# Turning the second tile's normed rows on chip: one edit to a hybrid decoder layer in float32

## The chip, the cores and the metric

The kernel runs on one core of one Trainium2 chip. A core has TensorE (PE, matrix products and 128x128 transposes), VectorE (DVE), ScalarE (ACT), GpSimd (POOL) and SyncE (SP), which work at the same time and wait for each other through semaphores. Transfers between the chip's memory (DRAM here) and the on-chip buffers go through 16 DMA engines; SP, ACT and POOL can issue them, each from its own queue in program order. The metric is the device time of one execution in microseconds; less is better. It is the median of 3 runs.

## What is computed

One decoder layer on 2048 tokens of 1024 channels in float32: a mixing half (RMS norm, one input projection, sliding-window attention, a convolution group, an output projection, RMS norm, residual) and then a SwiGLU half. Only the passage between the halves and the SwiGLU half matter here:

```
h  = h + rms_norm(mixed, mix_post_g)
hn = rms_norm(h, ffn_pre_g)
ff = (silu(hn @ w_gate) * (hn @ w_up)) @ w_down
h  = h + rms_norm(ff, ffn_post_g)
```

## The kernel before, in words

**Tiles and pairs.** The tokens are cut into 4 tiles (w = 0 to 3) of 512 tokens, and the SwiGLU half works on pairs: tiles 0 and 1, then tiles 2 and 3. Each pair's product with the weights is a 2 by 2 block product done with 7 block products in place of 8 (Winograd's form). Its right-hand operands are made from the normed rows `hn`, turned so that channels lie on partitions: B11 and B21 are the lower and upper 512 channels of the pair's first tile, B12 and B22 those of its second tile, and T1 = B12 - B11, T2 = B22 - T1, T3 = B22 - B12, T4 = B21 - T2. Each operand is 4 column blocks k = 0 to 3 of 128 channels by 512 tokens. For exactness each is split into a high part (a copy by ACT) and a low part (a subtraction by DVE, `lo`), and one float32 product becomes 3 matmuls; a block product (`product`) is 4 blocks x 3 = 12 matmuls of 128x512.

**Stages.** `stage_a` projects the inputs, `stage_b` does attention, `stage_taps` and `stage_tail` the convolution, `stage_w` the output projection, and `norm_w`, at its end, both norms of a tile. `stage_pre` (label F) then does the products that need only the pair's first tile (B11 for one half of its steps, B21 for the other): 40 for the first pair, of which the first 8 are done inside `stage_w(1)`, and 32 for the second. `stage_p1` does the others, which need T1, T2, T3, B22 and T4 in this order; `stage_p2` (label G) is the product with `w_down`, whose results go through `finish` (norm, residual from `h_scr`, output).

**How the second tile's rows get turned.** `norm_w` leaves four tiles `xs` of normed rows (128 tokens x 1024 channels each). For the first tile of a pair (w = 0 and 2) `turn_row` takes a block k: four transposes on PE into a PSUM bank, a copy by ACT that applies the gain `g_ffn` into a `gb` buffer, and a DMA into `hT` in DRAM. For the second tile (w = 1 and 3) the four `xs` are written to `hn_scr` in DRAM (L797, ACT's queue). `stage_h_sums` (label H) later loads from it, per k, two column strips of 128 channels (`load_cols`, L820), turns them with PE (`turned`, L842, banks of the pool `tr`), and makes r and t, the sums that become T1 to T4, with 4 `scalar_tensor_tensor` straight from PSUM and one subtraction on DVE; ACT copies B12 and B22 out of PSUM (L885, L887). The first tile's blocks come back from `hT` as `own` (L879).

**Buffers.** `BUFS` (L64 on) sets how many buffers a tag has. Those that matter: `chl` has 5, `mid` 4, `hl` 8, `gb` 2, `raw` 2 (weights, two products' worth each); PSUM has 4 `mm` banks, 3 `tr`, and one `ct`, which `turn_row` uses. `chl` holds, one after the other: `gb` (gain rows) and the four `xs` of `norm_w`, the four `ht` rows that `finish` loads from `h_scr` (L1141), then `own`, `r` and `t` of the sums, then `r1`, `s12`, `s34` of `stage_p1`. The accumulators of `stage_w(1)` and `stage_w(3)` are `mid`.

**Order of the work.** The Python code emits instructions into a main line (`run`) and into lanes: a lane emits a step of its item when the main line's clock has moved on by so much; `lh.rates` and the conditions in `add` set pace and start, `until` forces an item out. Emission order is priority only. The compiler then simulates the program and fixes each engine's order, and with it the order in SP's queue: a DMA whose buffer is not free holds up those behind it, also the weights' (`raw`, L931). The lane `lh` does the sums of the first pair as `S0`, from the step `P0.22` of `stage_pre` on at rate 0.9, and those of the second as `S2`, from `P2.16` on.

Of the kernel before, what the change touches and what calls it, by code (L numbers as in the profile page):

```python
# [12 lines left out]
F32 = mybir.dt.float32  # L13
# [4 lines left out]
AF = mybir.ActivationFunctionType  # L18
ALU = mybir.AluOpType
# [3 lines left out]
S = 2048  # L23
D = 1024
DFF = 2816
P = 128
T = 512
# [10 lines left out]
def layer_kernel(ctx, tc, x, xT, cols, rows, sinks, relb, onehot, w_in, w_pw, w_out, w_gate, w_up, w_down, out):  # L38
    nc = tc.nc
# [39 lines left out]
    act = nc.scalar.activation  # L79
# [38 lines left out]
    stt = dve(nc.vector.scalar_tensor_tensor)  # L118
    vtt = dve(nc.vector.tensor_tensor)
# [74 lines left out]
    ident = cst.tile([P, P], F32, name="ident")  # L194
# [16 lines left out]
    g_ffn = colt[:, 8:16]  # L211
# [27 lines left out]


    glu_scr = dr.tile([4, P, S], F32, name="glu_scr")
    hn_scr = dr.tile([S, D], F32, name="hn_scr")
# [517 lines left out]
    def norm_w(w, acc):  # L760
        L = f"W{w}"
        lab[0] = L

        def whole(src):
            t = f4("chl")
            nc.sync.dma_start(t, src)
            return t

        gb = whole(rows[0].partition_broadcast(P))
        ssq = sm(4)  # L770
        for s in range(4):
            act(junk, acc[s], AF.Square, accum_out=ssq[:, s : s + 1])
            yield 0.75
            lab[0] = L
        r = rsqrt(ssq, 4, D, w < 3)
        xs = [whole(x[w * T + s * P : w * T + (s + 1) * P]) for s in range(4)]
        ssq2 = sm(4)
        yield 3
        for s in range(4):
            lab[0] = L  # L780
            stt(acc[s], acc[s], r[:, s : s + 1], gb, ALU.mult, ALU.mult)
            yield 1.25
            lab[0] = L
            vtt(acc[s], xs[s], acc[s], ALU.add)
            r0 = w * T + s * P
            nc.sync.dma_start(h_scr[r0 : r0 + P], acc[s])
            act(junk, acc[s], AF.Square, accum_out=ssq2[:, s : s + 1])
            yield 1.25
        lab[0] = L
        r2 = rsqrt(ssq2, 4, D, w < 3)  # L790
        yield 3
        for s in range(4):
            lab[0] = L
            act(xs[s], acc[s], AF.Copy, scale=r2[:, s : s + 1])
            if w % 2:
                r0 = w * T + s * P
                nc.scalar.dma_start(hn_scr[r0 : r0 + P], xs[s])  # L797
            yield 1.25
        if w == 0:
            normed.extend(xs)  # L800
        if w == 2:
            for k in range(KC):
                turn_row(w, xs, k)
                yield 2.0

    normed = []

    def turn_row(w, xs, k):
        lab[0] = f"H{w}"
        b = ct()  # L810
        for s in range(4):
            nc.tensor.transpose(b[:, s * P : (s + 1) * P], xs[s][:, k * P : (k + 1) * P], ident)
        u = f2("gb")
        act(u, b, AF.Copy, scale=g_ffn[:, k : k + 1])
        nc.scalar.dma_start(hT[w // 2][k], u)
        return u

    def load_cols(w, k, tag):
        t = f2(tag, (P, 4, P))
        nc.sync.dma_start(t, hn_scr[w * T : (w + 1) * T, k * P : (k + 1) * P].rearrange("(s p) c -> p s c", p=P))  # L820
        return t

    def split_f(x, w):
        act(w[:, 0], x, AF.Copy)  # L824
# [2 lines left out]
    def lo(x, w, on_pool):  # L827
        (ptt if on_pool else vtt)(w[:, 1], x, w[:, 0].bitcast(F32), ALU.subtract)
# [1 line left out]
    OPTAG = {  # L830
        0: dict(B11=["x"] * 4, B21=["hl"] * 4, T1=["mid", "mid", "mb", "mb"], T2=["ql"] * 4, T3=["p"] * 4,
                T4=["yt", "yt", "mid", "mid"], B22=["hl"] * 4),
        2: dict(B11=["ql"] * 4, B21=["mid"] * 4, T1=["hl"] * 4, T2=["hl"] * 4, T3=["x"] * 4,
                T4=["yt", "yt", "mb", "mb"], B22=["p"] * 4),
    }
    COLTAG = {0: ["fc", "at", "fc", "at"], 2: ["fc", "at", "fc", "at"]}

    def turned(w, k, bank_of, tag):
        c = load_cols(w, k, tag)
        b = bank_of()  # L840
        for s in range(4):
            nc.tensor.transpose(b[:, s * P : (s + 1) * P], c[:, s], ident)  # L842
        return b
# [12 lines left out]
    def stage_h_plain(ws, ops, n, off):  # L856
        L = f"H{ws[0]}"
        for k in range(4):
            lab[0] = L
            if ws[0]:  # L860
                u = f2(COLTAG[ws[0]][k])
                nc.sync.dma_start(u, hT[ws[0] // 2][k + off])
            else:
                u = turn_row(0, normed, k + off)
                lab[0] = L
            o = op_tile(ws, ops, n, k, {})
            act(o[:, 0], u, AF.Copy)
            lo(u, o, False)
            yield 2.0

    def stage_h_sums(ws, ops):
        L = f"H{ws[0]}"
        spare = {}
        for k in range(4):
            lab[0] = L
            ct_ = COLTAG[ws[0]]
            g1, g2 = g_ffn[:, k : k + 1], g_ffn[:, k + 4 : k + 5]
            own = t_("chl", (P, 2, T))
            nc.sync.dma_start(own, hT[ws[0] // 2][k :: 4].rearrange("j p t -> p j t"))  # L879
            own = own[:, 0], own[:, 1]  # L880
            b12 = turned(ws[1], k, tr, ct_[2])
            b22 = turned(ws[1], k + 4, tr, ct_[3])
            r = t_("chl", (P, 2, T))
            t = t_("chl", (P, 2, T))
            act(r[:, 1], b12, AF.Copy, scale=g1)  # L885
            b = op_tile(ws, ops, "B22", k, spare)
            act(b[:, 0], b22, AF.Copy, scale=g2)  # L887
            yield 1.5
            lab[0] = L
            stt(r[:, 0], b12, g1, own[0], ALU.mult, ALU.subtract)  # L890
            stt(t[:, 0], b22, g2, r[:, 0], ALU.mult, ALU.subtract)
            stt(r[:, 1], b22, g2, r[:, 1], ALU.mult, ALU.subtract)
            stt(b[:, 1], b22, g2, b[:, 0].bitcast(F32), ALU.mult, ALU.subtract)
            vtt(t[:, 1], own[1], t[:, 0], ALU.subtract)
            yield 3
            for n, x in (("T1", r[:, 0]), ("T2", t[:, 0]), ("T3", r[:, 1]), ("T4", t[:, 1])):
# [406 lines left out]
    def since(lane, name, dt):  # L1303
        return name in lane.done and clk[0] >= lane.done[name] + dt
# [55 lines left out]
    W_LEAD = 4.0  # L1360
    RT = 0.2
    RP = 0.1
    NS = 12
    TIE = 5
    AHEAD = 3
    PRES = {0: 20, 2: 16}
    Q0 = 8
    POOL_LO = (3, 6)
    PRE_S0, PRE_S2 = 22, 16
# [7 lines left out]
    lu = Lane(0.6, 0)  # L1377
    ld = Lane(2.0, 0)
    lanes = [lb, lc, lu, lw, ld, lf, lh, lt]
    lh.rates = {"N1": 1.2, "S0": 0.9, "H0": 1.2}  # L1380
    lf.rates = {n: 0.6 for n in ("O0.1", "O0.3", "E0.1", "E0.3")} | {n: 1.2 for n in ("Y0", "Y1", "O2.1", "O2.3")}
    lc.rates = {"T0": RC0, "T1": RC1, "T2": RC2, "T3": RP}
    lw.rates = {"W0": RW0, "C2": RW, "W2": RW, "C3": RW, "W3": RW}
# [63 lines left out]
    ws, ops = (0, 1), {}  # L1447
# [12 lines left out]
    ws, ops = (2, 3), {}  # L1460
# [76 lines left out]
```

## Time and profile before

| what | before |
|---|---|
| median of 3 runs | 1987.95 us (1983.87 to 1989.76) |
| the profiled execution's own time | 1988.28 us |
| its span in the trace | 1986.6 us |
| TensorE busy | 1933.8 us, 97% of the span |
| VectorE busy | 1469.8 us, 74% |
| ScalarE busy | 957.8 us, 48% |
| GpSimd busy | 292.4 us, 15% |
| mean DMA rate over the span | 224 GB/s |

Times in the trace count from the start of the span. A row of windows has the window, its length, then for PE, PEld (weight loads), DVE, ACT and POOL the busy time with the number of instructions, the clock that PE was granted (1.00 is full), the busy share of the DMA engines and GB/s. A row of the timeline has start, duration, engine (SPq and ACTq are the issuing queues), line, instruction, written tile and read tiles with the stage's label behind @, the number merged, and in brackets how long the engine idled before and what released it. Rows of a tile's view have min, median and max duration in ns and the first and last start. Matmuls overlap in their pipeline, so that PE counts as busy at less than its full rate: the number of matmuls in a window says more than the busy time.

### The profile page before, as it was taken

The page shows a single profiled execution, that of the slowest core. Times are in us where ns is not written, and L with a number is a line of the kernel's source. Part 1 is how long each engine was busy: PE and PEld are TensorE (multiplying, and loading weights), DVE is VectorE, ACT ScalarE, POOL GpSimd, SP SyncE. Part 2 cuts the span into 40 slices and gives each one's busy share as a digit, 9 for nine tenths or more (in the row PEclk, how much of TensorE's full clock was granted, in tenths as well). Part 3 has the DMA queues.
Part 4 walks back from the last instruction along what each step waited for, and adds up shares of the span by engine and source line. Part 5 has one row for each costly group of instructions (what it writes and reads, how often), then busy time and mean ns, then how long its engine had stood idle before and what let it go on. Part 6 is the DMA issues. An engine that isn't in the chain of part 4 may idle for free.

```text
span 1986.6 us, 26668 instructions
## 1 busy us (share of the span) xinstructions
PE 1933.8 (97%) x8730; PEld 1549.4 (78%) x8730; DVE 1469.8 (74%) x2648; ACT 957.8 (48%) x1878; POOL 292.4 (15%) x427
## 2 busy tenths in 40 slices
PE   8999999999998999989999999998999999999997
PEld 6777777777776788778888878886788888888886
DVE  4999969995875898787759965667866665455557
ACT  5455454447646643334345464656643433345443
POOL 4011111111121011220000100000023332311003
PEclk9999999999998999999999999999999999999999
DMA  8786667566659777785478776769844442466664
GB/s 304 251 311 214 211 192 251 181 211 218 221 196 324 267 253 241 252 279 172 140 253 275 256 272 229 249 219 372 295 148 163 170 151 83 143 226 198 212 194 145
DMA packets 219180, 444.07 MB, mean 224 GB/s; under 512 B 22137, under 2 KB 47905, under 8 KB 219041
## 3 DMA queue, kind: packets, MB, share of 16 engines
q1 hardware_dynamic: 200096, 406.71, 61.3%
q0 software_dynamic: 7040, 23.07, 3.4%
q10 hardware_dynamic: 11904, 12.59, 1.8%
q8 instruction: 68, 1.11, 0.2%
q14 instruction: 72, 0.58, 0.1%
HBM read 327.46 MB, written 114.83 MB: 223 GB/s over the span
## 4 chain that ended last, share of the span: by engine, by line
PE 75%; DMA 10%; DVE 9%; issue 3%; ACT 2%; POOL 1%; SPq 0%; DVEq 0%; POOLq 0%; ACTq 0%
PE mm@F L85 30%; PE mm@G L85 16%; PE mm@A L85 14%; PE mm@W L85 5%; PE tr@B L85 4%; DVE fc@C L94 3%; PE tr@W L85 2%; DMA raw@F<-w_gate 1%; PE mm@U L85 1%; DMA chl@G<-h_scr 1%; DMA gb@F<-keeps 1%; DMA td<-wx@G 1%; DVE w@F L94 1%; DMA raw@F<-w_up 1%; DMA raw@A<-w_in 1%
## 5 line engine op out<-in xcount | busy, mean ns | idle before, releaser
L94 DVE SCALAR_TENSOR_TENSOR fc@C<-glu@C,colt,fc@C 128x512 f32<-128x512 f32 x480 | 357.2, 758 | 2.8
L85 PE MATMUL mm@F<-hl@H,w@F 128*128 128x512 f32 x1056 | 259.1, 397 | 8.4 <-ACT mm@F L954 7.8
L85 PEld LDWEIGHTS mm@F<-hl@H,w@F 128*128 128x128 f32 x1056 | 202.2, 192 | 53.1 <-ACT mm@F L954 9.2
L85 PE MATMUL mm@G<-hl@G,hl@G 128*128 128x512 f32 x924 | 227.4, 393 | 1.1 <-DVE hl@G L94 1.1
L824 ACT ACTIVATE w@F<-chl@F 128x512 fp32r<-128x512 f32 x220 | 136.0, 625 | 175.0 <-PE mm@F L85 170.1
L85 PE MATMUL mm@A<-hl@A,w@A 128*128 128x512 f32 x840 | 207.9, 395 | 4.7 <-ACT w@A L127 1.8
L85 PEld LDWEIGHTS mm@G<-hl@G,hl@G 128*128 128x128 f32 x924 | 171.7, 188 | 37.6 <-DVE hl@G L94 1.9
L85 PE MATMUL mm@G<-w@G,hl@G 128*128 128x512 f32 x876 | 199.4, 389 | 0.0
L85 PEld LDWEIGHTS mm@G<-w@G,hl@G 128*128 128x128 f32 x876 | 164.4, 188 | 34.1
L85 PEld LDWEIGHTS mm@A<-hl@A,w@A 128*128 128x128 f32 x840 | 155.4, 188 | 42.9 <-issue 3.1
L94 DVE TENSOR_TENSOR w@F<-chl@F,w@F 128x512 fp32r<-128x512 f32 x198 | 147.4, 747 | 32.9 <-ACT w@F L824 32.5
L85 PE MATMUL mm@F<-mid@H,w@F 128*128 128x512 f32 x528 | 138.9, 412 | 13.4 <-ACT mm@F L954 10.0
L85 PEld LDWEIGHTS mm@F<-mid@H,w@F 128*128 128x128 f32 x528 | 104.8, 200 | 38.2 <-ACT mm@F L954 11.4
L85 PE MATMUL mm@F<-ql@H,w@F 128*128 128x512 f32 x528 | 129.2, 390 | 0.7 <-DVE w@F L94 0.5
L85 PE MATMUL mm@F<-p@H,w@F 128*128 128x512 f32 x528 | 129.0, 390 | 0.0
L85 PE MATMUL mm@F<-x@H,w@F 128*128 128x512 f32 x528 | 126.9, 392 | 0.0
L85 PEld LDWEIGHTS mm@F<-ql@H,w@F 128*128 128x128 f32 x528 | 99.2, 188 | 22.1 <-DVE w@F L94 0.9
L85 PEld LDWEIGHTS mm@F<-p@H,w@F 128*128 128x128 f32 x528 | 99.2, 188 | 20.6
L85 PEld LDWEIGHTS mm@F<-x@H,w@F 128*128 128x128 f32 x528 | 98.5, 188 | 21.0 <-issue 0.8
L127 ACT ACTIVATE w@A<-raw@A 128x512 fp32r<-128x512 f32 x110 | 67.6, 626 | 92.2 <-PE mm@A L85 62.6
L94 DVE TENSOR_TENSOR w@G<-raw@G,w@G 128x512 fp32r<-128x512 f32 x73 | 52.0, 713 | 67.8 <-ACT w@G L824 66.9
L495 POOL TENSOR_SCALAR_AFFINE_SELECT p@B<-p@B 128x512 f32<-128x512 f32 x62 | 52.4, 854 | 337.6 <-ACT p@B L493 336.2
(303 smaller groups left out, 3267.9 us busy)
## 6 DMA issues: line engine op xcount, KB each, us to landing
mids<-fa@F SPq DMA_DIRECT2D x154, 256.0 KB, 3.1
raw@A<-w_in SPq DMA_DIRECT2D x55, 512.0 KB, 4.5
w@A<-lo_in SPq DMA_DIRECT2D x84, 256.0 KB, 3.4
fc@G<-mids SPq DMA_DIRECT2D x77, 256.0 KB, 3.5
fa@G<-mids SPq DMA_DIRECT2D x75, 256.0 KB, 4.8
gb@F<-keeps SPq DMA_DIRECT2D x72, 256.0 KB, 4.2
w@W<-fold SPq DMA_DIRECT2D x32, 512.0 KB, 5.3
chl@F<-w_gate SPq DMA_DIRECT2D x22, 512.0 KB, 4.3
```

The lines of the kernel that those rows point to most:

```text
L85: r = nc.tensor.matmul(*args, **kw)
L94: r = op(*args, **kw)
L127: act(w[:, 0], raw, AF.Copy)
L495: nc.gpsimd.affine_select(out=pg[:, kb].rearrange("p (i q) -> p i q", q=P), in_=pg[:, 1].rearrange("p (i q) -> p i q", q=P), compare_op=AL ...
L824: act(w[:, 0], x, AF.Copy)
```

## The change

`hn_scr` is gone. `norm_w` of the second tile of a pair goes on, after its last scaling, with 8 turns: for k = 0 to 3 it takes a `mid` buffer and turns the blocks k and k + 4 into its two halves with `turn_row`, so that the gain is applied by the copy. The four buffers are kept in `normed`. `stage_h_sums` takes the buffer of its k, and makes the four sums on DVE from on-chip buffers, in `own` and in one more `chl` buffer `r` (`t` is gone); the copy of B22 is now a plain copy, and its low part the usual subtraction. The DMA into `hT` moves from `turn_row` to its callers. Second pair: B21 goes into `hl` buffers and T1 into `mid` (they were the other way round). In the lanes: `S0` starts when `N1` (the norm of tile 1 with its 8 turns) has been emitted, at rate 0.8; `B21.2` starts at `P2.0` at rate 0.5; `S2` starts at `P2.8` if `E0.3` (the last `finish` of the first pair) has been emitted, at rate 0.8.

```
         for s in range(4):
             act(xs[s], acc[s], AF.Copy, scale=r2[:, s : s + 1])
-            if w % 2:
-                r0 = w * T + s * P
-                nc.scalar.dma_start(hn_scr[r0 : r0 + P], xs[s])
             yield 1.25
         if w == 0:
             normed.extend(xs)
-        if w == 2:
+        elif w == 2:
             for k in range(KC):
-                turn_row(w, xs, k)
+                u = turn_row(w, xs, k, f2("gb"))
+                nc.scalar.dma_start(hT[1][k], u)
                 yield 2.0
+        else:
+            for k in range(4):
+                t = t_("mid", (P, 2, T))
+                for j in range(2):
+                    turn_row(w, xs, k + 4 * j, t[:, j])
+                    yield 2.0
+                normed.append(t)
...
-        2: dict(B11=["ql"] * 4, B21=["mid"] * 4, T1=["hl"] * 4, T2=["hl"] * 4, T3=["x"] * 4,
+        2: dict(B11=["ql"] * 4, B21=["hl"] * 4, T1=["mid"] * 4, T2=["hl"] * 4, T3=["x"] * 4,
...
             own = t_("chl", (P, 2, T))
-            nc.sync.dma_start(own, hT[ws[0] // 2][k :: 4].rearrange("j p t -> p j t"))
-            own = own[:, 0], own[:, 1]
-            b12 = turned(ws[1], k, tr, ct_[2])
-            b22 = turned(ws[1], k + 4, tr, ct_[3])
-            r = t_("chl", (P, 2, T))
-            t = t_("chl", (P, 2, T))
-            act(r[:, 1], b12, AF.Copy, scale=g1)
-            b = op_tile(ws, ops, "B22", k, spare)
-            act(b[:, 0], b22, AF.Copy, scale=g2)
-            yield 1.5
-            lab[0] = L
-            stt(r[:, 0], b12, g1, own[0], ALU.mult, ALU.subtract)
-            stt(t[:, 0], b22, g2, r[:, 0], ALU.mult, ALU.subtract)
-            stt(r[:, 1], b22, g2, r[:, 1], ALU.mult, ALU.subtract)
-            stt(b[:, 1], b22, g2, b[:, 0].bitcast(F32), ALU.mult, ALU.subtract)
-            vtt(t[:, 1], own[1], t[:, 0], ALU.subtract)
-            yield 3
+            nc.sync.dma_start(own, hT[ws[0] // 2][k::4].rearrange("j p t -> p j t"))
+            other = normed[k]
+            yield 2.5
+            lab[0] = L
+            b = op_tile(ws, ops, "B22", k, spare)
+            act(b[:, 0], other[:, 1], AF.Copy)
+            r = t_("chl", (P, 2, T))
+            vtt(r[:, 0], other[:, 0], own[:, 0], ALU.subtract)
+            vtt(r[:, 1], other[:, 1], r[:, 0], ALU.subtract)
+            vtt(own[:, 0], other[:, 1], other[:, 0], ALU.subtract)
+            lo(other[:, 1], b, False)
+            vtt(own[:, 1], own[:, 1], r[:, 1], ALU.subtract)
+            yield 2
...
-    lh.rates = {"N1": 1.2, "S0": 0.9, "H0": 1.2}
+    lh.rates = {"N1": 1.2, "S0": 0.8, "B21.2": 0.5, "S2": 0.8}
...
-    lh.add("S0", stage_h_sums(ws, ops), lambda: f"P0.{PRE_S0}" in started and "B3" in lb.done)
+    del normed[:]
+    lh.add("S0", stage_h_sums(ws, ops), lambda: "N1" in lh.done)
...
-    lh.add("B21.2", stage_h_plain(ws, ops, "B21", 4), lambda: since(lw, "N3", NS))
-    lh.add("S2", stage_h_sums(ws, ops), lambda: f"P2.{PRE_S2}" in started)
+    del normed[:4]
+    lh.add("B21.2", stage_h_plain(ws, ops, "B21", 4), lambda: "P2.0" in started)
+    lh.add("S2", stage_h_sums(ws, ops), lambda: f"P2.{PRE_S2}" in started and "E0.3" in lf.done)
```

More of the change, by code (lines that the diff above doesn't have):

```diff
@@ L241, in layer_kernel @@
     glu_scr = dr.tile([4, P, S], F32, name="glu_scr")
-    hn_scr = dr.tile([S, D], F32, name="hn_scr")
     y_scr = dr.tile([4, P, S], F32, name="y_scr")
@@ L800, in norm_w, with turn_row @@
             normed.extend(xs)
-        if w == 2:
+        elif w == 2:
             for k in range(KC):
-                turn_row(w, xs, k)
+                u = turn_row(w, xs, k, f2("gb"))
+                nc.scalar.dma_start(hT[1][k], u)
                 yield 2.0
+        else:
[5 more added lines that the diff above has]
+                normed.append(t)
     normed = []
-    def turn_row(w, xs, k):
+    def turn_row(w, xs, k, u):
         lab[0] = f"H{w}"
@@ L812, in turn_row @@
             nc.tensor.transpose(b[:, s * P : (s + 1) * P], xs[s][:, k * P : (k + 1) * P], ident)
-        u = f2("gb")
         act(u, b, AF.Copy, scale=g_ffn[:, k : k + 1])
-        nc.scalar.dma_start(hT[w // 2][k], u)
         return u
[L818 to L821, printed above, removed]
     def split_f(x, w):
@@ L836, in layer_kernel @@
     COLTAG = {0: ["fc", "at", "fc", "at"], 2: ["fc", "at", "fc", "at"]}
[L838 to L843, printed above, removed]
     def op_tile(ws, ops, n, k, spare):
@@ L863, in stage_h_plain @@
             else:
-                u = turn_row(0, normed, k + off)
+                u = turn_row(0, normed, k + off, f2("gb"))
                 lab[0] = L
+                nc.scalar.dma_start(hT[0][k + off], u)
             o = op_tile(ws, ops, n, k, {})
@@ L875, in stage_h_sums @@
             lab[0] = L
-            ct_ = COLTAG[ws[0]]
-            g1, g2 = g_ffn[:, k : k + 1], g_ffn[:, k + 4 : k + 5]
             own = t_("chl", (P, 2, T))
-            nc.sync.dma_start(own, hT[ws[0] // 2][k :: 4].rearrange("j p t -> p j t"))
-            own = own[:, 0], own[:, 1]
-            b12 = turned(ws[1], k, tr, ct_[2])
-            b22 = turned(ws[1], k + 4, tr, ct_[3])
-            r = t_("chl", (P, 2, T))
-            t = t_("chl", (P, 2, T))
-            act(r[:, 1], b12, AF.Copy, scale=g1)
-            b = op_tile(ws, ops, "B22", k, spare)
-            act(b[:, 0], b22, AF.Copy, scale=g2)
-            yield 1.5
-            lab[0] = L
-            stt(r[:, 0], b12, g1, own[0], ALU.mult, ALU.subtract)
-            stt(t[:, 0], b22, g2, r[:, 0], ALU.mult, ALU.subtract)
-            stt(r[:, 1], b22, g2, r[:, 1], ALU.mult, ALU.subtract)
-            stt(b[:, 1], b22, g2, b[:, 0].bitcast(F32), ALU.mult, ALU.subtract)
-            vtt(t[:, 1], own[1], t[:, 0], ALU.subtract)
-            yield 3
-            for n, x in (("T1", r[:, 0]), ("T2", t[:, 0]), ("T3", r[:, 1]), ("T4", t[:, 1])):
+            nc.sync.dma_start(own, hT[ws[0] // 2][k::4].rearrange("j p t -> p j t"))
[4 more added lines that the diff above has]
+            act(b[:, 0], other[:, 1], AF.Copy)
+            r = t_("chl", (P, 2, T))
+            vtt(r[:, 0], other[:, 0], own[:, 0], ALU.subtract)
[4 more added lines that the diff above has]
+            yield 2
+            for n, x in (("T1", r[:, 0]), ("T2", r[:, 1]), ("T3", own[:, 0]), ("T4", own[:, 1])):
                 lab[0] = L
@@ L1362, in layer_kernel @@
     RP = 0.1
-    NS = 12
     TIE = 5
@@ L1368, in layer_kernel @@
     POOL_LO = (3, 6)
-    PRE_S0, PRE_S2 = 22, 16
+    PRE_S2 = 8
     H1, H2, H3, H4 = 0, 4, 7, 11
```

## The prediction

> **What bounds the kernel now.** I read the page first, then who PE waits for, then windows over the two passages that the change touches, and the timelines of each engine in them.
>
> ```profile
> span 1986.6 us, 26668 instructions
> PE 1933.8 (97%) x8730; PEld 1549.4 (78%) x8730; DVE 1469.8 (74%) x2648; ACT 957.8 (48%) x1878; POOL 292.4 (15%) x427
> ...
> PE mm@F L85 <- ACT mm@F L954: 17.8, 7, 4.2
> ```
>
> PE sets the time: whatever doesn't let PE start a matmul earlier is worth nothing. Its longest wait, 17.8 us in 7 pieces, is in `stage_pre`, for the copy that seeds a PSUM bank. All 7 lie in two windows, from about product 11 of the first pair and product 0 of the second up to the first product of `stage_p1`. A window of undisturbed work stands beside them.
>
> ```profile
> 587.50:685.29 97.79, 89.22 (x378) 72.22 (x377) 69.46 (x105) 61.24 (x107) 6.11 (x14) 0.93 0.88 291
> 1321.82:1432.88 111.06, 98.96 (x417) 79.71 (x416) 87.97 (x187) 75.47 (x146) 1.28 (x1) 0.92 0.99 347
> 1455.00:1555.00 100.00, 100.00 (x443) 82.83 (x442) 70.75 (x84) 38.44 (x67) 35.00 (x23) 1.00 0.48 164
> ```
>
> Undisturbed, a matmul takes 100/443 = 0.2257 us. Each of the two windows has 32 transposes, in 8 groups at about 0.4 us a group (below). So the first needs 346 x 0.2257 + 3.2 = 81.3 us and takes 97.8; the second needs 385 x 0.2257 + 3.2 = 90.1 and takes 111.1. **16.5 and 21.0 us are lost**, 37.5 in all. The DMA engines are 0.88 and 0.99 busy there, against 0.48 undisturbed. Part of the loss is clock: 24 matmuls behind a wait of 3.76 us take 8.33 us, where 24 x 0.2257 = 5.4.
>
> ```profile
> 624.27 8.54 PE L85 MATMUL mm@F<-hl@H,w@F 128*128 128x512 f32 x24 [3.41 <-ACT mm@F L954]
> ...
> 685.29 1.52 PE L85 MATMUL mm@F<-ql@H,w@F 128*128 128x512 f32 x6
> ...
> 1386.33 8.33 PE L85 MATMUL mm@F<-mid@H,w@F 128*128 128x512 f32 x24 [3.76 <-ACT mm@F L954]
> ...
> 1432.88 7.87 PE L85 MATMUL mm@F<-hl@H,w@F 128*128 128x512 f32 x34
> ```
>
> The rows at 685.29 and 1432.88 are the first products of `stage_p1`; they are the two dates that count.
>
> **What goes.**
>
> ```profile
> hn_scr<-chl@W ACTq DMA_DIRECT2D x8, 512.0 KB, 7.1
> ...
> fc@H<-hn_scr SPq DMA_DIRECT2D x8, 256.0 KB, 5.4
> at@H<-hn_scr SPq DMA_DIRECT2D x8, 256.0 KB, 5.4
> ```
>
> 4 MB go in and 4 MB out of `hn_scr`, 4.2 MB per pair in decimal units. In the second window, where the DMA engines move 347 GB/s and have no room, that is 12.1 us of transfer, and up to 12.1 of its 21.0 us can come back. In the first, with 0.88, PE would be the limit without them and all 16.5 can come back. If nothing new stood in the way, the sum would be -16.5 - 12.1 = -28.6 us.
>
> **What the work costs.** The transposes are 32 per pair before and after. The next rows have DVE and ACT.
>
> ```profile
> L94 DVE SCALAR_TENSOR_TENSOR chl@H<-tr@H,colt,chl@H 128x512 f32<-128x512 f32 x24 | 17.2, 746 | 4.5 <-ACT chl@H L885 2.9 <-DMA chl@H<-hT 0.7 <-DVE chl@H L94 0.5
> L94 DVE TENSOR_TENSOR chl@H<-chl@H,chl@H 128x512 f32<-128x512 f32 x8 | 5.5, 685 | 0.0
> ...
> L814 ACT ACTIVATE gb@H<-ct@H,colt 128x512 f32<-128x512 f32 x16 | 11.0, 686 | 11.2 <-PE ct@H L812 11.1
> L885 ACT ACTIVATE chl@H<-tr@H,colt 128x512 f32<-128x512 f32 x8 | 5.4, 676 | 3.3 <-DVE p@G L94 3.3
> ...
> L867 ACT ACTIVATE hl@H<-gb@H 128x512 fp32r<-128x512 f32 x4 | 2.5, 630 | 0.8 <-ACT gb@H L814 0.8
> ```
>
> DVE does 5 subtractions per k, 5 x 0.685 = 3.4 us, in place of 4 x 0.746 + 0.685 = 3.7: 1 us less per pair. ACT has 8 turn copies of 0.686 for 8 of 0.676, and 4 plain copies of 0.63 more: 2.6 us more per pair. Both are busy for 61 to 88 us of the windows' 98 and 111, so I cost this at 0; without that cover it would be +2.6 - 1 per pair. The swap of `hl` and `mid` costs 0: `hl` comes free with the last step of `stage_p2` at 1321.8, and B21 isn't needed before the 17th product, 16 x 12 x 0.2257 = 43 us on. The rates and conditions only set priorities. They count where two ready instructions compete, so I keep +-1 us for them.
>
> **What is late next: the turns.** `turn_row` has one PSUM bank, `ct`. Each turn is PE, then ACT, then PE again, and this row of steps shows how fast that goes while PE is full of matmuls: the turns of tile 2, those of tile 0, and those of the convolution, which have no DMA behind them.
>
> ```profile
> 1171.74 0.60 PE L812 MATMUL ct@H<-ident,chl@W 128*128 128x128 f32 x4
> ...
> 1205.92 0.60 PE L812 MATMUL ct@H<-ident,chl@W 128*128 128x128 f32 x4
> ...
> 494.90 0.66 PE L812 MATMUL ct@H<-ident,chl@W 128*128 128x128 f32 x4
> ...
> 535.58 0.60 PE L812 MATMUL ct@H<-ident,chl@W 128*128 128x128 f32 x4
> ...
> 1217.09 0.60 PE L550 MATMUL ct@C<-ident,fc@C 128*128 128x128 f32 x4
> 1222.54 0.60 PE L550 MATMUL ct@C<-ident,fc@C 128*128 128x128 f32 x4
> 1228.03 0.60 PE L550 MATMUL ct@C<-ident,fc@C 128*128 128x128 f32 x4
> ```
>
> From the first to the last are 6 steps of tile 2 in 34.2 us, 5.7 each; 7 of tile 0 in 40.7, 5.8 each; the convolution's 5.5. The work in a step is 0.4 + 0.7 us; the rest is the place in PE's order behind some 23 matmuls. I take 5.7 for the new turns. The other end is 1.5 us, if PE turned back at once.
>
> The last scaling ends here:
>
> ```profile
> 611.98 1.14 ACT L794 ACTIVATE chl@W<-mid@W,sm@W 128x1024 f32<-128x1024 f32 x1
> ...
> 1339.76 1.14 ACT L794 ACTIVATE chl@W<-mid@W,sm@W 128x1024 f32<-128x1024 f32 x1
> ```
>
> The 8th turn then comes at 613.1 + 1 + 7 x 5.7 = 654 and at 1381.8. Until then all four `xs` are read, so 4 of 5 `chl` buffers are held. Before, they came free when `hn_scr` was written, some 7 us after the scaling.
>
> **First pair.** The fifth buffer has `own` for k = 0, and `r` must wait for an `xs`:
>
> ```profile
> 592.29 0.37 SPq L879 DMA_DIRECT2D chl@H<-hT  x1
> ...
> 634.06 2.25 DVE L94 SCALAR_TENSOR_TENSOR chl@H<-tr@H,colt,chl@H 128x512 f32<-128x512 f32 x3 [2.90 <-ACT chl@H L885]
> ...
> 637.48 0.69 DVE L94 TENSOR_TENSOR chl@H<-chl@H,chl@H 128x512 f32<-128x512 f32 x1
> 638.08 0.68 DVE L94 TENSOR_TENSOR ql@H<-chl@H,ql@H 128x512 fp32r<-128x512 f32 x1
> ...
> 665.77 0.69 DVE L94 TENSOR_TENSOR mb@H<-chl@H,mb@H 128x512 fp32r<-128x512 f32 x1
> ```
>
> So the sums would begin not sooner but later: at about 656, where they now begin at 634.06. From there to the last block of T1 took 32.4 us with PE stalling; 33 DVE operations, one every 0.60 us, are 20 at the least, with DVE's work for the products between them. I take 26, the middle: T1 at 682, first product of `stage_p1` at 683. PE is through with `stage_pre` at 587.5 + 81.3 = 669 and then stands for 14 us in one piece; behind that I charge the slow clock once, 8.33 - 5.4 = 2.9. Against 685.29 that is +0.6; I take **+1**, with -5 (20 us) and +7 (32.4) as ends. The waits go from the middle of the passage to its end. The weights' loads aren't late any more, but that is now hidden.
>
> A rule of the Trainium skill prices the clock in another way: "TensorE: Matmul & The Clock Gate", Part 1, states that an idle window of about 3.4 us halves the clock until about 3.4 us of sustained work have gone by. By it, one long stop would cost 1.7 us, however long, and both heads together 2.4 us less than in my sum, 1981. The rows of 8.54 and 8.33 us show 2.9 to 3.1.
>
> **Second pair.** The residual loads of `finish` stand ahead of `own` for the same buffers:
>
> ```profile
> 1340.38 0.91 SPq L1141 DMA_DIRECT2D chl@G<-h_scr  x1
> ...
> 1342.64 3.26 SPq L1141 DMA_DIRECT2D chl@G<-h_scr  x2
> ...
> 1377.78 0.75 DVE L94 SCALAR_TENSOR_TENSOR chl@H<-tr@H,colt,chl@H 128x512 f32<-128x512 f32 x1 [0.72 <-DMA chl@H<-hT]
> ...
> DMA to landing us min/median/max: 3.2/6.4/9.0
> ```
>
> The last row is the landing of these loads. After the change, one buffer is left for them until 1382: the second load at 1340.4, then one per 6.4 us of landing and about 2 of use, so the sixth is done at 1382. The last two and `own` go out together, 2.1 MB, 6 us at 347 GB/s, and the sums begin at about 1391 against 1377.78. With 26 us and 3 for four last operations of `finish` (0.75 each) T1 is there at 1420 and `stage_p1` begins at 1421. PE would be at the end of `stage_pre` at 1321.8 + 90.1 = 1412, and waits 9. With 2.9 for the clock and 3 for weights held back by the burst at 1382 that is 1427, **-6** against 1432.88. Behind a load that waits for its buffer, SP's queue holds the weights, and PE waits for these. The ends are -12 (all that the traffic is worth) and +8 (each wait as the last rival has it, but half as long).
>
> **Sum.** 1988.3 for the profiled execution, +1, -6: **1983.3**, I say 1983. The median shown is 1987.95, 0.3 us lower, which is nothing here. 0.3%, or 6 us, is about the least that a measurement of this kernel can tell from no change. So I forecast a change too small to tell, on the faster side of nothing.
>
> **Rivals.** *Quick turns* (0.18): the order puts transposes behind few matmuls; at 1.5 us a step the `xs` come free at 625 and 1352, the sums begin before the old dates, and the traffic that is gone counts in full: 1988.3 - 28.6 = 1960. For it speaks that PE stalls less when turns have priority; against it three rows of turns at 5.5 to 5.8.
>
> *Residual loads hold the weights* (0.33): in the second pair, six loads go through one buffer one after the other, and each stands in SP's queue for as long as the one at 1342.64 did, 3.26 us, because real landings are later than the order assumed. That is 6 x 3.26 = 19.6 us, in which weights come late, PE's turns stretch, and the sums with them: `stage_p1` at 1421 + 19.6 + 2.9 = 1443.5, +10.6; with +1 from the first pair 2000. It turns the sign once these waits pass 9 us in all, and shows beyond 0.3% past 16. For it speaks the 3.26 itself; against it that only this one load waited so, when two were held at once.
>
> *It doesn't do what it says* (0.03): the traffic that is gone is taken up by other transfers, the dates stay, 1988.
>
> **How the numbers follow.** The forecast case has 0.46. Its ends added up are 1988.3 - 5 - 12 = 1971 and 1988.3 + 7 + 8 = 2003; as the two pairs hardly reach them together, I take 1974 to 1998 as its own range. Of its 0.46, 0.19 lies below 1982, 0.22 within 0.3% and 0.05 above 1994. Faster: 0.19 + 0.18 for the quick turns = 0.37. Within 0.3%: 0.22 + 0.03 = 0.25. Slower: 0.05 + 0.33 for the loads = 0.38. The range runs from 1962, short of most of the quick turns (0.12 left out), to 2006, past the loads' 2000 (0.08 left out).
>
> **What would show it.** In the changed profile, look at the `ct@H` groups behind the last scaling near 612 and 1340: 5 to 6 us apart is the forecast, 1 to 2 the first rival. The first subtraction into `chl@H` should come at about 656 and 1391. PE should wait little for the seeds of `stage_pre` and 9 to 14 us in one piece ahead of `stage_p1`. In the second pair, waits of SP over 3 us at L1141 point to the second rival. What would prove me wrong: sums that begin before 634 or 1378, or waits for seeds as large as now.

## The result and the profile after

The change makes the kernel slower. Its median is 1997.21 us (1995.37 to 2002.37, 5 runs) against 1987.95 (1983.87 to 1989.76, 5 runs): a ratio of 1.0064, 95% interval 1.0052 to 1.0075. The execution profiled after took 1997.21 us, 8.9 more than the one before. First the head of the page and PE's longest waits:

```profile
span 1995.5 us, 26639 instructions
PE 1931.1 (97%) x8730; PEld 1546.0 (77%) x8730; DVE 1467.7 (74%) x2648; ACT 961.7 (48%) x1886; POOL 296.0 (15%) x427
...
PE mm@F L85 <- ACT w@F L821: 13.4, 2, 12.6
PE mm@F L85 <- ACT mm@F L939: 9.0, 5, 3.0
PE mm@F L85 <- DVE fa@F L94: 7.5, 2, 5.9
```

The wait for seeds (now L939) went from 17.8 to 9.0 us: from 7.8 to 1.9 in the first pair, but only from 10.0 to 7.1 in the second. A new one of 12.6 us in one piece stands at the top, in the first pair, and it waits for a weight, not for an operand. Next the windows of the two passages, from the same points as before (product 12 of the first pair and product 0 of the second, each up to the first product of `stage_p1`), with the same columns:

```profile
586.90:683.87 96.97, 82.50 (x378) 67.46 (x377) 65.37 (x100) 62.45 (x106) 10.07 (x22) 0.95 0.82 265
1331.55:1435.76 104.21, 96.14 (x417) 76.77 (x416) 79.46 (x173) 71.67 (x142) 0.00 (x0) 0.97 0.89 310
```

The first passage takes 97.0 us for 97.8, the second 104.2 for 111.1; the DMA engines are less busy in both. So up to the first products of `stage_p1` the change has won 7.7 us. The loss lies behind them. PE's steps around these dates:

```profile
620.83 0.60 PE L816 MATMUL ct@H<-ident,chl@W 128*128 128x128 f32 x4
621.19 5.69 PE L85 MATMUL mm@F<-hl@H,w@F 128*128 128x512 f32 x24
...
655.22 0.60 PE L816 MATMUL ct@H<-ident,chl@W 128*128 128x128 f32 x4
655.58 15.69 PE L85 MATMUL mm@F<-hl@H,w@F 128*128 128x512 f32 x68
683.87 1.22 PE L85 MATMUL mm@F<-mid@H,w@F 128*128 128x512 f32 x2 [12.61 <-ACT w@F L821]
688.09 2.07 PE L85 MATMUL mm@F<-mid@H,w@F 128*128 128x512 f32 x4 [2.99 <-DVE w@F L94]
...
1395.95 7.14 PE L85 MATMUL mm@F<-hl@H,w@F 128*128 128x512 f32 x23 [2.96 <-ACT mm@F L939]
1402.93 0.60 PE L816 MATMUL ct@H<-ident,chl@W 128*128 128x128 f32 x4
...
1413.45 7.34 PE L85 MATMUL mm@F<-hl@H,w@F 128*128 128x512 f32 x24 [2.91 <-ACT mm@F L939]
1421.04 13.90 PE L85 MATMUL mm@F<-hl@H,w@F 128*128 128x512 f32 x60 [0.24 <-ACT mm@F L939]
1435.76 0.73 PE L85 MATMUL mm@F<-mid@H,w@F 128*128 128x512 f32 x2 [0.83 <-ACT w@F L821]
1439.31 4.64 PE L85 MATMUL mm@F<-mid@H,w@F 128*128 128x512 f32 x10 [2.81 <-DVE w@F L94]
```

In the first pair the turns are 24 matmuls and 5.7 us apart, and PE stands 12.61 us ahead of `stage_p1`. In the second pair it stands there for 0.83 us only: it is busy with `stage_pre` until 1434.9. At the head of `stage_p1` PE does two matmuls and waits again, for the next weight, in both pairs. DVE and SP's queue show why, for the first:

```profile
655.11 0.54 DVE L94 TENSOR_SCALAR fc@C<-glu@C,colt 128x512 f32<-128x512 f32 x1
...
656.17 0.68 DVE L94 TENSOR_TENSOR chl@H<-mid@W,chl@H 128x512 f32<-128x512 f32 x1
656.78 0.74 DVE L94 SCALAR_TENSOR_TENSOR fc@C<-glu@C,colt,fc@C 128x512 f32<-128x512 f32 x1
...
681.27 0.67 DVE L94 TENSOR_TENSOR mb@H<-chl@H,mb@H 128x512 fp32r<-128x512 f32 x1
...
682.48 0.68 DVE L94 TENSOR_TENSOR chl@F<-chl@F 128x512 f32<-128x512 f32 x1
```
```profile
675.84 0.33 SPq L993 DMA_DIRECT2D chl@F<-w_gate  x1
...
685.35 0.39 SPq L993 DMA_DIRECT2D chl@F<-w_up  x1
```

The first sum comes at 656.17, the last block of T1 (`mb@H`) at 681.27. `chl@F` are weights: `stage_p1` loads half of each weight (L993) and makes its weight sums in the same five `chl` buffers. The first load goes out at 675.84, when the operands' sums free a buffer, so that the weight, not T1, is last.

Three stretches show where each kernel wins and loses. They are counted in matmuls of `stage_pre`, `stage_p1` and `stage_p2` from the first one of the first pair: A from matmul 0 to 600 (480 of `stage_pre`, then 120 of `stage_p1`), B from 600 to 2772 (the rest of the first pair), C from 2772 to 3216 (second pair: 384 of `stage_pre`, 60 of `stage_p1`). Behind C all kernels take the same time (540.1 to 540.4 us). The chips differed by up to 5 us (the kernel before had medians of 1988.0, 1983.7, 1985.5, 1983.0 and 1984.4 us), so ratios are to the kernel before on the same chip. The stretches come from one profiled execution each. Two executions of one kernel, e3_old_lanes and e3_again, lie 1.3, 1.7 and 2.7 us apart in them, on two chips, and against the row before, up to 5 us of a row's sum can be the chip's. The rows changed and before are from the same chip, and so are e13 and e14.

| kernel | ratio, 95% interval | A | B | C |
|---|---|---|---|---|
| before | 1 | 202.0 | 609.3 | 124.7 |
| changed | 1.0064, 1.0052 to 1.0075 | 207.8 | 613.9 | 123.6 |
| after_again | 1.0060, 1.0044 to 1.0077 | 206.0 | 613.3 | 122.9 |
| e1_three_banks | 0.9962, 0.9947 to 0.9977 | 198.4 | 605.0 | 119.9 |
| e2_r_elsewhere | 0.9960, 0.9946 to 0.9975 | 192.3 | 608.7 | 119.8 |
| e3_old_lanes | 1.0006, 0.9990 to 1.0022 | 204.8 | 609.2 | 124.4 |
| e3_again | 1.0001, 0.9989 to 1.0013 | 203.5 | 607.5 | 121.7 |
| e4_traffic | 0.9966, 0.9955 to 0.9977 | 195.0 | 604.5 | 125.1 |
| e5_taps_late | 1.0033, 1.0019 to 1.0048 | 199.1 | 617.1 | 124.5 |
| e6_weights_elsewhere | 1.0011, 0.9998 to 1.0023 | 200.0 | 617.6 | 117.4 |
| e12 | 1.0026, 1.0013 to 1.0040 | 199.0 | 611.9 | 125.2 |
| e7_banks_traffic | 1.0054, 1.0036 to 1.0072 | 203.5 | 616.1 | 125.8 |
| e9_new_lanes_only | 1.0117, 1.0098 to 1.0136 | 205.0 | 619.9 | 135.0 |
| e10_r_old_lanes | 0.9963, 0.9949 to 0.9977 | 198.5 | 606.4 | 120.3 |
| e13_s0_old | 0.9998, 0.9982 to 1.0013 | 204.7 | 605.9 | 119.1 |
| e14_s2_old | 1.0049, 1.0031 to 1.0067 | 207.7 | 611.5 | 123.7 |

The change lost 5.8 us in A and 4.5 in B, and won 1.1 in C: 9.2 in all.

### The profile page after: what moved, and what is told of

The parts are those of the page before. It is cut to its first block, busy times and chain, and to the rows that moved or that the text cites. A ratio compares the mean times of both kernels' runs of the same rounds, so it can differ in the third digit from the quotient of the medians.

```text
span 1995.5 us, 26639 instructions
## 1 busy us (share of the span) xinstructions
PE 1931.1 (97%) x8730; PEld 1546.0 (77%) x8730; DVE 1467.7 (74%) x2648; ACT 961.7 (48%) x1886; POOL 296.0 (15%) x427
## 4 chain that ended last, share of the span: by engine, by line
PE 80%; DMA 8%; DVE 7%; issue 2%; POOL 1%; ACT 1%; SPq 0%; DVEq 0%; POOLq 0%; ACTq 0%
PE mm@F L85 33%; PE mm@G L85 17%; PE mm@A L85 14%; PE mm@W L85 5%; PE tr@B L85 4%; PE tr@W L85 3%; PE mm@U L85 1%; DMA mids<-fa@F 1%; DMA gb@F<-keeps 1%; DMA raw@F<-w_gate 1%; DVE fc@C L94 1%; DMA td<-fc@G 1%; PE tr@B L491 1%; DVE w@F L94 1%; DMA fc@G<-w_down 1%
```

## The experiments

The theory (H) was that the slow turns hold `chl`, and that everything late follows from that. Its rivals: the new lane starts and rates cost the time (L), or VectorE is full whenever the sums come (D). Later one more came up: the weights of `stage_p1` wait for `chl`. The kernel after_again is the changed kernel once more, on a chip with experiments.

> The changed kernel itself once more, on the chip that timed the other experiments, as the yardstick for them. The kernel before has 1983.7 us there. If the 0.64% hold from chip to chip, this gives 1983.7 x 1.0064 = 1996 us, and the kernels with faster turns (1975.0) and with r elsewhere (1973.9) are 21 and 22 us better than the change as made. If the difference belongs to a chip, it comes out near 1984, and those two are worth 9 and 10 us.

The 0.6% hold from chip to chip: 1.0060.

**e1_three_banks.** The second tile's turns take turns through the three `tr` banks.

```
-        b = ct()
+        b = tr() if w % 2 else ct()
```

> The second tile's turns use the pool tr (three banks) in place of the one bank ct; nothing else changes. Theory H (slow turns through one bank hold four chl buffers, so the sums come late and PE stands ahead of stage_p1): turns at most 3 us apart, first sum before 635, no PE wait over 4 us ahead of stage_p1 in the first pair, 1970 us (1962 to 1982). Rival L (the new starts and rates of the lanes cause the loss): no change, 1993 to 2001. Rival D (VectorE is full there whenever the sums come): sums earlier, but stage_p1 within 4 us of where it is, 1990 to 1998.

It is 0.4% faster than before and 1.0% faster than the change. PE's timeline:

```profile
620.56 1.47 PE L816 MATMUL tr@H<-ident,chl@W 128*128 128x128 f32 x12
621.79 4.83 PE L85 MATMUL mm@F<-hl@H,w@F 128*128 128x512 f32 x20
626.46 1.04 PE L816 MATMUL tr@H<-ident,chl@W 128*128 128x128 f32 x8
...
676.06 2.43 PE L85 MATMUL mm@F<-ql@H,w@F 128*128 128x512 f32 x10
```

Two or three turns now stand together and the last is through at 627.5, 28 us sooner. The first sum starts at 630.8, and PE runs from `stage_pre` into `stage_p1` without a stop. The slow turns were the cause of the late sums.

**e2_r_elsewhere.** The turns stay slow; the sum `r` leaves `chl`.

```
-            r = t_("chl", (P, 2, T))
+            r = (f2("fc"), f2("at"))
```

> r goes into one fc and one at buffer in place of a chl buffer; the turns stay on one bank, 5.7 us apart. H: in the first pair the sums of k = 0 begin near 622 in place of 656 and stage_p1 some 10 us sooner; in the second pair own still waits behind the loads from h_scr, so little there: 1986 us (1980 to 1992). L: no change, 1993 to 2001. D: 1990 to 1998.

0.9960, with the best A of all.

```profile
616.81 0.68 DVE L94 TENSOR_TENSOR fc@H<-mid@W,chl@H 128x512 f32<-128x512 f32 x1
```
```profile
654.72 0.60 PE L816 MATMUL ct@H<-ident,chl@W 128*128 128x128 f32 x4
...
669.08 3.02 PE L85 MATMUL mm@F<-hl@H,w@F 128*128 128x512 f32 x12 [1.25 <-ACT mm@F L939]
672.26 0.74 PE L85 MATMUL mm@F<-ql@H,w@F 128*128 128x512 f32 x2 [0.16 <-ACT w@F L821]
```

The last turn is as late as ever (654.72), but the sums begin at 616.81, behind the first turns. So it isn't the turns as such that cost time: it is the buffers they hold.

**e3_old_lanes and e3_again.** The change with the lane starts and rates of before; run a second time for a more typical trace.

```
-    lh.rates = {"N1": 1.2, "S0": 0.8, "B21.2": 0.5, "S2": 0.8}
+    lh.rates = {"N1": 1.2, "S0": 0.9, "H0": 1.2}
-    lh.add("S0", stage_h_sums(ws, ops), lambda: "N1" in lh.done)
+    lh.add("S0", stage_h_sums(ws, ops), lambda: "P0.22" in started and "B3" in lb.done)
-    lh.add("B21.2", stage_h_plain(ws, ops, "B21", 4), lambda: "P2.0" in started)
-    lh.add("S2", stage_h_sums(ws, ops), lambda: f"P2.{PRE_S2}" in started and "E0.3" in lf.done)
+    lh.add("B21.2", stage_h_plain(ws, ops, "B21", 4), lambda: since(lw, "N3", 12))
+    lh.add("S2", stage_h_sums(ws, ops), lambda: "P2.16" in started)
```

> The changed kernel with the old starts and rates of the lanes (S0 from P0.22 at 0.9 and after B3, B21.2 after N3 and 12, S2 from P2.16 at 0.9). H: the turns and buffers are the same, so 1997 us (1991 to 2002). L: back to 1988 or below.

> The kernel with the old lane starts and rates once more, because the trace taken of it the first time was its slowest run of ten (1993.5 for a median of 1984.4). Theory 'the lanes cost time in the middle': again 0 to 0.2% above the kernel before, some 0.5% below the changed kernel, and the stretch from the third round of stage_p1 of the first pair to product 0 of the second pair, which costs the changed kernel 4.0 to 4.5 us against the kernel before, costs 0 here. Theory 'scatter': near the changed kernel's 1.006, and the middle costs as much as there.

1.0006 and 1.0001: the new way of the rows alone changes nothing that can be measured, and the 0.6% of the change belong to its lane edits. In the second trace B is 1.8 us below before, where the change has 4.5 above; part of the difference can be the chip's.

**e13_s0_old and e14_s2_old.** Each takes back one half of the lane edits: the start and rate of `S0` (first pair), or those of `B21.2` and `S2` (second pair).

> The changed kernel with the old start and rate of S0 alone, the first pair's sums; the second pair's lanes stay new. Theory 'the first pair's lane costs the time': all of the 0.6% goes, 0.9995 to 1.001 as with all old lanes; the sums for w_down and the taps come later against the sums of the operands, T1 is ready 3 us sooner, and the stretch from the third round of stage_p1 to the second pair costs 4 to 6 us less than in the changed kernel. Theory 'the second pair's lanes cost it': 1.004 to 1.007.

> The changed kernel with the old starts and rates of B21.2 and S2 alone, the second pair's sums; S0 stays new. Theory 'the first pair's lane costs the time': as the changed kernel, 1.0045 to 1.0065; from product 0 of stage_pre to the first product of stage_p1 the second pair needs 102 to 104 us in both. Theory 'the second pair's lanes cost it': 1.000 to 1.002.

0.9998 and 1.0049: it is `S0`, its start and its rate together; the two weren't taken apart. Held against each other on their one chip, e13 is 3.0, 5.6 and 4.6 us ahead of e14 in A, B and C. DVE in e13_s0_old, to be held against the rows of the change above:

```profile
655.42 1.41 DVE L94 TENSOR_TENSOR chl@H<-mid@W,chl@H 128x512 f32<-128x512 f32 x2
...
661.84 0.54 DVE L94 TENSOR_SCALAR fc@C<-glu@C,colt 128x512 f32<-128x512 f32 x1
...
678.12 0.69 DVE L94 TENSOR_TENSOR mb@H<-chl@H,mb@H 128x512 fp32r<-128x512 f32 x1
```

The sums begin within 0.8 us of the same date, but T1 is ready 3.2 us sooner. The convolution's taps (`fc@C`) are held back until `S0` has been emitted (`lc.hold`, L1435); an earlier `S0` lets them go earlier. Up to T1's last block DVE does 8 taps and 4 sums for `w_down` in the change, 4 and 3 here: 5 operations of some 0.65 us. That is the 3 us of stretch A. In B, PE's waits for `fa@F` go with `S0` too: from 740 to 1020 us they are 7.5 us in the change, 7.7 in after_again and 7.9 in e14, but 3.4 before, 2.2 in e13 and 1.9 in e3_again. The largest in the change is this one, in PE's, DVE's and SP's timelines:

```profile
817.05 2.92 PE L85 MATMUL mm@F<-mid@H,w@F 128*128 128x512 f32 x6 [5.89 <-DVE fa@F L94]
```
```profile
813.58 0.69 DVE L94 TENSOR_TENSOR chl@F<-chl@F 128x512 f32<-128x512 f32 x1 [4.92 <-DMA chl@F<-w_gate]
```
```profile
803.29 0.33 SPq L991 DMA_DIRECT2D raw@F<-w_up  x1
806.29 0.33 SPq L993 DMA_DIRECT2D chl@F<-w_gate  x1
```

DVE stands before a weight sum whose load was issued only at 806.29, and the DVE operation on `fa@F` that PE waits for comes behind it. Why the order with the early `S0` has this load so late wasn't found out, nor was the difference in C, which is in the second pair, followed up.

**e5_taps_late.** Taps and `w_down` sums wait for the 20th product of `stage_p1`.

```
+            started.add(f"Q{ws[0]}.{q}")
...
-    lc.hold = lambda: "S0" not in lh.done
+    lc.hold = lambda: "Q0.20" not in started
...
-    lt.add("TS", stage_tsums(td))
+    lt.add("TS", stage_tsums(td), lambda: "Q0.20" in started)
```

> The convolution's taps and the sums for w_down wait until the 20th product of stage_p1; the turns keep their 23 to 24 matmuls between them, and the first subtraction into chl@H its date of about 656. Theory 'VectorE full': of its operations from 655 to 690, 10 are taps and 6 are w_down sums, 16 x 0.62 = 10 us. So T1 is ready 6 to 10 us sooner, the first product of stage_p1 comes at 674 to 678 for 683.9, the first two rounds lose nothing for 6.6 us, and the time falls by 10 to 15 us, less what the taps cost later (up to 4). Theory 'weights of stage_p1 wait for chl': the first product follows only as far as the buffers come free sooner, 3 to 5 us, the second weights are still late, and the loss of the first rounds stays at 4 to 6; -3 to -6 us in all. Theory 'only the late turns count': no change, within 3 us.

With the turns as slow as in the change, the first product of `stage_p1` comes at 676.5, 7.4 us sooner: the 12 operations above, at 0.62 each. 'VectorE full' is right at this place. But against the change A wins 7 to 9 us and B loses 3 to 4, and the kernel ends only 0.3% faster. That DVE must do what it has put off while `stage_p1` needs it is the likely reason for B, but wasn't shown.

**e6_weights_elsewhere.** The first weight of `stage_p1` and its sums S1 and S2 go into `fc` and `at`.

```
+                if m == 0:
+                    r1 = (f2("fc"), f2("at"))
+                    for a in range(2):
+                        nc.sync.dma_start(r1[a], src1[:, a])
...
+                if m == 0:
+                    r["S1"], r["S2"] = f2("fc"), f2("at")
```

> The first step of stage_p1 takes its second weight block and the sums S1 and S2 from the buffers fc and at and no longer from chl, in both pairs; turns and sums as in the changed kernel. Theory 'weights wait for chl': the load of the first weights no longer stands at 675.8, the first product comes with T1 at 682 (-2), the second weights aren't late, so that the 6.6 us of the first rounds and the 5.8 us of the second pair mostly go: -8 to -14 us. Theory 'VectorE full': the operations are the same and VectorE does them no sooner: within 3 us of the changed kernel. Theory 'only the late turns count': the same, within 3 us.

0.5% faster than the change, as 'weights wait for chl' has it. PE's timeline:

```profile
670.32 1.07 PE L85 MATMUL mm@F<-ql@H,w@F 128*128 128x512 f32 x4
...
677.80 0.50 PE L85 MATMUL mm@F<-mb@H,w@F 128*128 128x512 f32 x1 [2.40 <-ACT mb@H L884]
...
682.51 0.80 PE L85 MATMUL mm@F<-ql@H,w@F 128*128 128x512 f32 x1 [3.44 <-ACT ql@H L884]
```

PE begins `stage_p1` 13.6 us sooner and then waits for late blocks of T1 and T2 (`mb@H`, `ql@H`): weights and sums were late together, and each hid the other. In C, 5.5 to 6.2 us go; the first 60 matmuls of `stage_p1`, with the second wait at 1439.31 among them, had lost the change 5.9. In B it is 3.7 to 4.2 us slower than the change, which wasn't followed up.

**e7_banks_traffic and e4_traffic.** All writes and reads of `hn_scr` are put back as extra work that nobody uses, in e1_three_banks and in the changed kernel.

```
+                nc.scalar.dma_start(hn_scr[r0 : r0 + P], xs[s])
...
+            for tag, kk in (("fc", k), ("at", k + 4)):
+                c = f2(tag, (P, 4, P))
+                nc.sync.dma_start(c, hn_scr[w * T : (w + 1) * T, kk * P : (kk + 1) * P].rearrange("(s p) c -> p s c", p=P))
```

> Turns in the three tr banks as in the kernel that ran at 0.9962 of the kernel before, and all writes and reads of hn_scr put back as extra work that nobody uses (8.4 MB). Theory 'the traffic itself cost time', as the prediction had it: up to 12.1 us come back in the second pair and some in the first, 0.9962 + 0.006 = 1.002 or more. Theory 'only the dates at which chl comes free count': the turns and sums keep their dates, and the time stays within 0.2% of 0.9962.

> The changed kernel with all transfers through hn_scr put back as extra work that nobody uses: xs written to it, and per k two column strips read into fc and at buffers. H with the relief due to the missing traffic: the 30th product of the first pair, 15.5 us early in the changed kernel, comes some 10 us later again, but stage_p1 begins where it does now, since PE waits there for the sums: 1998 us (1994 to 2004). If the relief came from the sums having moved out of stage_pre and not from the traffic: the 30th product stays within 3 us and 1997 us.

e7_banks_traffic is 0.9% slower than e1_three_banks: 5.1 us in A and 5.9 in C, where the transfers are, and 11 in B, where they are not. So more than the traffic differs between the two, and the 5.1 and 5.9 aren't a clean price of it. e4_traffic came out faster than the change, against every theory. Its PE timeline has the reason:

```profile
628.58 0.60 PE L820 MATMUL ct@H<-ident,chl@W 128*128 128x128 f32 x4
628.93 3.00 PE L85 MATMUL mm@F<-hl@H,w@F 128*128 128x512 f32 x12
631.77 0.60 PE L820 MATMUL ct@H<-ident,chl@W 128*128 128x128 f32 x4
```

With the extra transfers the compiler put 12 matmuls between most of the turns, not 24; the eighth turn starts at 639.75, the sums at 640.1. Without meaning to, it does what e1's edit does. In C, where its order has 23 to 27 between most turns, it is 1.5 to 2.2 us slower than the change.

**e9_new_lanes_only.** The kernel before with the change's lane starts and rates alone.

> The kernel before, with nothing of the change but the new starts and rates of the lanes; rows still go through hn_scr. Theory 'the lanes cost time': 0.3 to 0.6% slower than before, with DVE's waits in the middle of stage_p1 as in the changed kernel. Theory 'the lanes cost only where the sums wait for chl': the xs come free some 7 us after the scaling here, so the sums begin as early as their loads allow, before 634, and it is within 0.2% of before or up to 0.5% faster.

1.0117, worse than either theory said, with 3, 10.5 and 10.3 us lost in A, B and C. The lane edits cost more without the new way of the rows than with it; why is open.

**e10_r_old_lanes** and **e12.** `r` elsewhere with all old lanes, and `r` elsewhere with three banks.

> r in fc and at, with the old starts and rates of the lanes. r elsewhere alone ran at 0.9960 of the kernel before. Theory 'chl and lanes are two separate costs': 0.9960 - 0.005 = 0.991. Theory 'old lanes only take back what late sums do to VectorE': with r elsewhere nothing of it is left, 0.995 to 0.998; as the sums then start only at P0.22, it may lose some of the 13 us that r elsewhere wins ahead of stage_p1, up to 1.000.

> Both edits together: turns in the three tr banks, and r in fc and at. Theory 'chl is held': each edit alone already takes sums off the late release of the xs buffers, so the two overlap, and this lies at the better of the two or a little below, 1969 to 1974 us on this chip (1975.0 and 1973.9 alone). Theory 'the turns themselves delay T1': with r elsewhere the sums of the last block still wait for the 8th turn (654.7); with quick turns T1 is ready by 655, and PE's waits for the seeds are what is left: 1964 to 1969.

0.9963: with `r` out of `chl` the lanes no longer matter (0.9960 with the new ones). e12, 1.0026, refutes its expectations: two edits that each gain 1.0% on the change gain 0.3% together. Its longest wait, and what ACT did ahead of it:

```profile
1392.45 7.99 PE L85 MATMUL mm@F<-hl@H,w@F 128*128 128x512 f32 x24 [8.13 <-ACT mm@F L939]
```
```profile
1385.65 0.63 ACT L873 ACTIVATE p@H<-mid@G 128x512 fp32r<-128x512 f32 x1 [2.88 <-DMA out<-p@G]
1389.06 0.63 ACT L884 ACTIVATE hl@H<-at@H 128x512 fp32r<-128x512 f32 x1 [2.78 <-DVE at@H L94]
...
1390.78 1.13 ACT L821 ACTIVATE w@F<-raw@F 128x512 fp32r<-128x512 f32 x2
1391.82 0.58 ACT L939 ACTIVATE mm@F<-gb@F 128x512 f32<-128x512 f32 x1
```

In ACT's order a B22 copy waits for `p`, which `finish` is still writing out, and the seed stands behind it. Here sums that come early hold up a seed. That is one place; A and B are up to 7 us worse than with one edit too, and that wasn't followed up.

No kernel beat e2_r_elsewhere: 0.9960 of the kernel before, and 1.0% under the change.

## Why the prediction was wrong

It forecast -5 us, too small to tell, on the faster side; +0.64% was measured. That the range holds it is luck: 0.33 of the 0.38 for a slower kernel was there for the residual loads, which did not hold anything up, and the step that failed was given +-1 us.

- **The failed step is "The rates and conditions only set priorities ... so I keep +-1 us for them."** The lane edits cost 0.6%, 12 us. e3 and e13 take them back, e13 those of `S0` alone, and give 1.0001 and 0.9998, too small to tell, as forecast for the whole. `S0` starts earlier, and with it opens the gate `lc.hold`, which the step did not look at; taps then stand among the sums. That accounts for the 3 us in A; how the rest comes about is open. e1 and e2 win more than this 0.6% with the new lanes in place, but they remove late sums, which the forecast had in its sum; the lanes it had not. Any edit also gives the compiler a new order, and e4, e9 and e12 came out far from every theory, so what an early `S0` costs in another kernel isn't shown.
- *PE's waits for seeds, which were to give way to one long wait ahead of `stage_p1`*: right in the first pair (7.8 to 1.9 us, and 12.61 in one piece), wrong in the second. There 7.1 of 10.0 us are left, `stage_pre` takes 103 us and not 90.1, and PE waits 0.83 us ahead of `stage_p1` and not 9. The seeds stand behind their own loads: from 1390 to 1436 ACT waits 7.9 us in 5 pieces for `gb@F<-keeps`; why these are late is open.
- *First pair: turns 5.7 us apart, `chl` held until 654, sums at 656, PE standing 14 us, `stage_p1` at 683*: right to about two microseconds (655.8, 656.17, 12.61, 683.87), and shown by e1 and e2. The rival of quick turns is what e1 built; it is worth 0.4%, some 8 us, not the 28.6 it was priced at; seeds still cost e1 15.0 us of waits.
- *The traffic is worth up to 12.1 us in the second pair*: at most half, as far as is known. C grew by 5.9 us when it was put back with quick turns (e7) and by 1.5 to 2.2 with slow ones (e4), and in both more than the traffic changed.
- *One charge of 2.9 us for the clock*, behind the first product: mis-sized. `stage_p1`'s weights also come through `chl`, so a second wait of 2.99 follows. The window of the first 24 matmuls:

```profile
683.87:695.93 12.06, 9.07 (x24) 6.72 (x25) 12.06 (x21) 4.46 (x8) 3.22 (x6) 0.58 0.70 229
```

  24 x 0.2257 is 5.4: 2.99 for the wait and 3.65 for the clock, 6.6 us in place of 2.9.
- *Second pair, -6*: the sign was right, the size was not (C: -1.1). Behind the first product 5.9 us were lost, just what the sum charges for the clock and for weights. But that product came 104.2 us after product 0, not 99: the last scaling ended 23 us after it, not 19, the eighth turn came 48 us after the scaling, not 41, and the sums began 82 us after product 0, not 69 (1413.66). The rival of residual loads was not it: all eight were issued in under half a microsecond each, and SP's queue did not stand before them:

```profile
L1126 SPq DMA_DIRECT2D chl@G<-h_scr x8: 326/384/451, 1333.7 to 1403.9; - x8
```

- *No term for the stretch between the two passages*: 4.5 us were lost in B. They go with `S0` (e13 is 5.6 us ahead of e14 there); how is open.

One sum of the prediction comes out otherwise: by its own terms, with the +1 of the first pair, waits for residual loads turn the sign of the whole at 8 us and pass 0.3% at 14, not at 9 and 16. Nothing rests on it.

## What to carry to other kernels

When rows no longer go through DRAM, ask for how long they now hold their buffers and who else uses that tag, weights as well as operands: here moving one temporary out of the shared tag was worth 1.0%. An edit of a start condition is an edit of everything that is gated on it; list the gates before pricing it at nothing. Two edits that each relieve the same queue need not add up, and extra work can help by changing the compiled order alone, so compare the order too.

## What the runs showed of the hardware

The length of a wait doesn't decide alone whether the clock falls. In the profile before, 12 matmuls behind a wait of 2.36 us take 4.62 us (2.7 at full speed); after the change, 6 behind 2.63 take 1.65 (1.4 at full speed):

```profile
647.21 4.62 PE L85 MATMUL mm@F<-hl@H,w@F 128*128 128x512 f32 x12 [2.36 <-ACT mm@F L954]
```
```profile
804.51 1.65 PE L85 MATMUL mm@F<-yt@H,w@F 128*128 128x512 f32 x6 [2.63 <-DVE at@F L94]
```

In all 16 traces the granted clock changes only on a grid of steps of 3.41 us; in the profile before it is 0.50 from 623.41 to 630.24, from 637.07 to 640.48 and from 647.31 to 650.72. Two windows before and two after, laid along the grid, show what counts:

```profile
643.89:647.30 3.41, 1.05 (x8) 0.69 (x6) 3.41 (x6) 2.85 (x6) 0.00 (x0) 1.00 0.91 278
647.31:650.72 3.41, 3.41 (x8) 2.67 (x9) 2.37 (x4) 2.52 (x5) 0.00 (x0) 0.50 0.81 231
```
```profile
799.75:803.16 3.41, 2.13 (x10) 1.43 (x8) 3.41 (x6) 0.00 (x0) 0.20 (x1) 1.00 0.01 5
803.16:806.58 3.42, 2.07 (x9) 1.73 (x10) 3.42 (x7) 0.89 (x2) 1.42 (x3) 1.00 0.74 244
```

The wait of 2.36 us lies in one step and leaves PE 1.05 us of work there, and the clock is 0.50 in the next. The wait of 2.63 us is split by the grid, each step keeps over 2 us of work, and the clock stays. Counted over the 16 traces, the clock fell 110 times; all but one of these falls stand behind a step in which PE was busy for less than 0.48 of it, and every step under 0.43 at full clock was followed by a fall. It rose again only behind steps that were over 0.83 busy. The one exception, in e3_old_lanes at 339.2 us, wasn't explained.

The Trainium skill ("TensorE: Matmul & The Clock Gate", Part 1) says that the gate's window of about 3.4 us runs freely, so that the moment of a change varies; the grid of 3.41 us agrees with that. In one point the rows differ from the rule as the prediction has it: a step need not be idle for the clock to fall, 1.05 us of work in it are too little. The waits of 3.41 and 3.76 us that the prediction read were followed by two slow steps each (623.41 to 630.24 is one such pair), so that they cost 2.9 to 3.1 us and not the 1.7 of one. After the change the clock was low for six steps, from 673.46 to 693.94, through both waits at the head of `stage_p1`: between them PE had two matmuls, too few to raise it.
